# Pairs of small experts: first product from whole float32 weights, tokens stationary on two column tiles

## The chip, the cores and the metric

The kernel runs on one core of a Trainium2 chip. The metric is the time of one execution on the device, in microseconds (us), the median over several executions. Single runs of the kernel before lay between 1557.11 and 1559.25 us.

TensorE is called PE in the profile (PEld is its loading of stationary operands), VectorE is DVE, ScalarE is ACT, GpSimd is POOL, and SyncE is SP, whose queue issues nearly all transfers.

## The reference, cut to what matters

One decoder layer on 512 tokens of width 1024: attention in two head groups, then a mixture of 32 experts of which each token takes 4, then a gated per-layer input and a norm. The change touches the mixture alone:

```python
def expert_block(args):
    e, xs = args
    hh = jnp.dot(xs, w_gu[e]) + b_gu[e]            # w_gu[e]: 1024 x 2048
    glu, lin = jnp.split(hh, 2, axis=-1)
    glu = jnp.minimum(glu, SWIGLU_LIMIT)
    lin = jnp.clip(lin, -SWIGLU_LIMIT, SWIGLU_LIMIT)
    act = glu * jax.nn.sigmoid(SWIGLU_ALPHA * glu) * (lin + 1.0)
    return jnp.dot(act, w_dn[e]) + b_dn[e]         # w_dn[e]: 1024 x 1024
```

All weights are float32: 12 MB for an expert.

## The kernel before, in words

The attention part lasts some 310 us and isn't touched. After it the experts are ordered by how many tokens they have, and each place in that order has a fixed capacity (`CAPS`, line 34): 128 tokens for the first six, falling to 64 for the last twelve. `RUNS` (line 42) lists the order of work. There are 26 runs, counted from 0: twenty with one expert each, and six pairs of two experts with 64 tokens each. The pairs are runs 1, 2, 6, 11, 18 and 25, the last. A run whose tokens don't fit is completed later by `overflow`.

**Weights.** An expert's weights are 12 chunks of 1 MB (128 partitions x 2 x 1024, `chunk_views`, line 738): q 0 to 3 are the gate half of the first product, 4 to 7 the linear half, 8 to 11 the down product. `jobs` (line 752) lists all chunks in the order of their loading; for a pair first expert 0's eight, then expert 1's eight, then the down chunks of both by turns. `issue` (line 774) gives each next chunk to a free one of 8 raw slots and issues the load on SP's queue; the load waits until the last reader of the slot is done. From run 23 on, two of the slots are kept for something else, so 6 are left. In run 25 four chunks of the later gate projection (`("t", q)`) stand in the list between the first product and the down product.

A chunk is then either split or native. `advance` (line 798) splits a chunk into two float16 parts, high and low, in two halves (`hl`, line 210: ACT writes the high part in line 212, DVE the low one in line 213), into one of 6 places (`HL`), and its raw slot is free again. `take` (line 826) runs splits up to `AHEAD` = 4 chunks past the one that is needed. Native chunks (`native`, line 766, by `NATIVE`, line 38: the last 4 of an expert with 64 tokens, the last 2 of other small ones) are multiplied as float32 from the raw slot, which is free after that (`done`, line 832).

**One run.** `prep` (line 1407) gathers the tokens by matmuls with one-hot matrices (`gather`, line 1232; line 1245) into `xT`, tokens along the free axis, in two float16 parts; this is written in the program between the first product and the down product of the run before. `up` (line 1268) does the first product for one expert: the bias (line 1279), then for each k and each of eight blocks of 128 outputs three matmuls (`mm3`, lines 218 to 220: high x high, low x high, high x low) with the weights stationary and the tokens moving; the result has outputs on partitions and tokens along the free axis. Gate and linear parts meet in lines 1298 to 1303. In a pair `up` runs twice, once for each expert. Then the down product: `down` (line 1307) for a single run, `down2` (line 1329) for a pair. `down2` takes whole float32 weights as moving operand, 512 columns at a time, and the activations as stationary operand; expert 0 writes PSUM partitions 0 to 63, expert 1 partitions 64 to 127, two column tiles of PE.

`y_out` (line 1341) scales the result into two float16 parts. Every third run, `combine` (line 1350) adds the results of the last three runs to the output by matmuls (line 1358); its eight pieces are spread over the first product of the next run by `step` (line 1366), one after each k. `at` (line 1415) puts small extra work (the sort, the down bias) at fixed points of some runs.

The framework may move instructions between places of the program where data allow; waits are kept by semaphores.

Of the kernel before, what the change touches and what calls it, by code (L numbers as in the profile page):

```python
# [19 lines left out]
P = 128  # L20
# [14 lines left out]
MAXBLK = 48  # L35
GROUP = 3
AHEAD = 4
NATIVE = {c: 0 if c == 128 else 4 if c <= 64 else 2 for c in CAPS}
SHIFT = 1200


# [7 lines left out]
def hybrid_layer(ctx: ExitStack, tc: tile.TileContext, x, p, positions, w_in, g_attn, g_cq, w_uq, g_ckv,  # L49
# [703 lines left out]
    for n_, us in enumerate(RUNS):  # L753

        if n_ == LAST - 1:
            jobs += [("t", 4), ("t", 5)]
        jobs += [(s_, q) for s_ in us for q in range(8)]
        if n_ == LAST:
            jobs += [("t", q) for q in range(4)]
        jobs += [(s_, q) for q in range(8, 12) for s_ in us]  # L760
# [546 lines left out]
    def down(y, get, put, acts, c):  # L1307

        split_acts = {}
        t = mp.tile([P, 2, 2, 4, P], F16, name="acts", bufs=1)  # L1310
        for q in range(4):
            slot, w = get(8 + q)
            j = q // 2
            if slot is not None and j not in split_acts:
                split_acts[j] = [t[:, j, b, :, :c] for b in range(2)]
                hl(*split_acts[j], acts[j], SX / S)
            for m in range(q % 2 * 2, q % 2 * 2 + 2):
                for n in range(2):
                    first, end = q == 0 and m == 0, q == 3 and m == 3
                    cols = slice(n * 512, (n + 1) * 512)  # L1320
                    if slot is None:
                        PE.matmul(y[n][:c], acts[j][:, m], w[:, m % 2, cols], start=first, stop=end,  # L1322
                                  skip_group_check=True)
                    else:
                        ah, al = split_acts[j]
                        mm3(y[n][:c], ah[:, m], al[:, m], w[0][:, m % 2, cols], w[1][:, m % 2, cols], first, end)
            put(8 + q)

    def down2(y, get, put, acts):

        for q in range(4):
            ws = [get(e, 8 + q)[1] for e in range(2)]
            for m in range(2):
                for n in range(2):
                    for e in range(2):
                        PE.matmul(y[n][e * 64:(e + 1) * 64], acts[e][:, 2 * q + m], ws[e][:, m, n * 512:(n + 1) * 512],  # L1336
                                  start=q + m == 0, stop=q + m == 4, skip_group_check=True)
            for e in range(2):
                put(e, 8 + q)

    def y_out(y, gcl, c):
        yh = mp.tile([P, D], F16, name="yh", tag="yh", bufs=4)
# [64 lines left out]
    def prep(us, between=None, mid=None):  # L1407
        n, s_ = len(us), us[0]
        pos, X_ = (posf, X3) if s_ < 2 else (XP, XS)
        oh = onehots(pos[:, :, s_:s_ + n], n * CAPS[s_], n)  # L1410
        if between is not None:
            between()
        return gather(oh, lambda i: X_[:, i, 0:2, s_:s_ + n], n * CAPS[s_], n, mid=mid)

    def at(ns_, k):
        for f in extra.pop((ns_, k), ()):
# [28 lines left out]
    for ns_, us in enumerate(RUNS):  # L1445
# [5 lines left out]
        if ns_ == LAST - 2:  # L1451
            later["keep"] = 2
        perm = st256 if us[0] < 2 else perm256
        acts = []

        def get(e, q):
            return take((us[e], q))

        def put(e, q):
            done((us[e], q))  # L1460

        for j in range(len(us)):
            acts += up(lambda q: get(j, q), lambda q: put(j, q), xT, j * c, perm[:, us[j]:us[j] + 1], c)
            at(ns_, j + 1)
        if len(us) == 1:
            at(ns_, 2)
        if ns_ + 1 < len(RUNS):
            nxt = prep(RUNS[ns_ + 1])
        y = [py_.tile([P, 512], F32, name="y", tag="py") for _ in range(2)]
        if ns_ == LAST:  # L1470
            step(99)
        if len(us) > 1:
            down2(y, get, put, acts)
        else:
            down(y, lambda q: get(0, q), lambda q: put(0, q), acts, c)
        at(ns_, 3)
# [121 lines left out]
```

## Time and profile before

| | |
|---|---|
| median of 3 executions | 1559.07 us |
| the profiled execution's own time | 1560.22 us |
| its span, first to last instruction | 1558.3 us |
| mean granted clock of PE | 0.97 of full speed |
| read from memory | 427.99 MB |
| mean rate over the span | 278 GB/s |

The span is the stretch that the trace shows, the profiled execution's own time has what lies around it. Runs 0 to 25 fill the trace from about 320 to 1492 us. In the views a row has a line of the kernel, an engine, an operation, what it writes and reads, and how often it stands there. Busy time of PE counts matmuls that overlap in the array once, so a busy PE need not be at its best rate; the number of matmuls in a stretch tells more. "Issue" is time in which an engine waited for nothing that the profile shows.

### The profile page before, as it was taken

How to read it: one execution, taken by the hardware profiler on the slowest of the kernel's cores; microseconds unless marked ns; L12 is line 12 of the kernel's file. 1: busy time of each engine (PE TensorE's matmuls, PEld its weight loads, DVE VectorE, ACT ScalarE, POOL GpSimd, SP SyncE). 2: the span in 40 equal slices, each digit the busy share in tenths (PEclk: the TensorE clock that was granted, in tenths of full speed). 3: DMA queues.
4: the chain of work that ended last, by engine and by line, in shares of the span. 5: the costliest groups of instructions: out<-in, count | busy, mean ns of one | idle time of the engine just before them, and what ended most of it. 6: DMA issues, size and time to landing. Idle time of an engine off the chain costs nothing. (4 is left out here: it accounts for less than half of the span.)

```text
span 1558.3 us, 44542 instructions
## 1 busy us (share of the span) xinstructions
PE 1401.5 (90%) x19286; PEld 1016.2 (65%) x19286; DVE 1175.4 (75%) x1624; ACT 980.8 (63%) x1393; POOL 45.0 (3%) x114
## 2 busy tenths in 40 slices
PE   7999899688889999899997999998987898899587
PEld 4766656486565787688776577676665566556447
DVE  7447876788595999599987387887857777788734
ACT  6458866567374887488675366766646646567534
POOL 2001000300000000000000000000000000000002
PEclk9999999889999999999999999999999899999799
DMA  7122131368899999799999699999987999788911
GB/s 246 46 85 83 55 109 44 119 227 277 317 399 368 408 407 344 267 382 408 342 356 349 216 405 367 399 334 344 351 312 290 391 354 340 279 322 317 330 69 55
DMA packets 124249, 433.00 MB, mean 278 GB/s; under 512 B 7977, under 2 KB 18770, under 8 KB 123986
## 3 DMA queue, kind: packets, MB, share of 16 engines
q1 hardware_dynamic: 123858, 429.85, 74.1%
q8 instruction: 153, 2.51, 0.6%
q14 instruction: 46, 0.38, 0.1%
q10 hardware_dynamic: 192, 0.26, 0.1%
HBM read 427.99 MB, written 2.10 MB: 276 GB/s over the span
## 5 line engine op out<-in xcount | busy, mean ns | idle before, releaser
L213 DVE SCALAR_TENSOR_TENSOR hl<-raw,hl 128x1024 f16<-128x1024 f32 x618 | 721.8, 1216 | 52.5 <-ACT hl L212 49.4
L212 ACT ACTIVATE hl<-raw 128x1024 f16<-128x1024 f32 x618 | 611.0, 1048 | 96.3 <-DMA raw<-in_w_gu_dram 57.8
L220 PE MATMUL hps<-xT,hl 128*128 128x64 f16 (+5 forms) x4096 | 501.2, 204 | 28.0 <-issue 13.4
L218 PE MATMUL hps<-xT,hl 128*128 128x64 f16 (+5 forms) x4096 | 504.6, 204 | 12.8 <-issue 11.1
L219 PE MATMUL hps<-xT,hl 128*128 128x64 f16 (+5 forms) x4096 | 503.7, 204 | 12.4 <-issue 12.4
L220 PEld LDWEIGHTS <-hl 128*128 128x128 f16 (+1 forms) x4208 | 400.3, 99 | 54.4 <-DVE hl L213 25.5
L219 PEld LDWEIGHTS <-hl 128*128 128x128 f16 (+1 forms) x4208 | 402.6, 99 | 38.7 <-issue 22.5
L218 PEld LDWEIGHTS <-hl 128*128 128x128 f16 (+1 forms) x4208 | 402.8, 99 | 33.9 <-issue 9.5
L1346 ACT ACTIVATE yh<-y,gcl 128x512 f16<-128x512 f32 (+4 forms) x52 | 35.1, 682 | 143.4 <-PE y L1336 69.3
L1347 DVE SCALAR_TENSOR_TENSOR yl<-y,gcl,yh 128x512 f16<-128x512 f32 (+4 forms) x52 | 38.3, 746 | 106.3 <-ACT yh L1346 104.4
L1336 PE MATMUL y<-raw,ln 128*64 128x512 f32 x384 | 101.2, 606 | 10.9 <-DVE ln L1299 10.4
L1247 ACT ACTIVATE xT<-pg 128x512 f16<-128x512 f32 (+4 forms) x104 | 53.1, 522 | 91.3 <-PE pg L1245 90.5
L1322 PE MATMUL y<-raw,ln 128*80 128x512 f32 (+3 forms) x224 | 98.6, 592 | 0.0
L218 PE MATMUL y<-hl,acts 128*128 128x512 f16 (+4 forms) x208 | 82.5, 397 | 5.9 <-ACT acts L212 5.6
L1358 PE MATMUL pg<-yh,ohT 128*128 128x512 f16 (+4 forms) x208 | 80.8, 389 | 7.0 <-issue 5.1
L219 PE MATMUL y<-hl,acts 128*128 128x512 f16 (+4 forms) x208 | 81.7, 393 | 0.0
L220 PE MATMUL y<-hl,acts 128*128 128x512 f16 (+4 forms) x208 | 79.3, 392 | 2.6 <-DVE acts L213 2.0
L1358 PE MATMUL pg<-yl,ohT 128*128 128x512 f16 (+4 forms) x208 | 80.6, 389 | 0.7 <-DVE yl L1347 0.6
L1336 PEld LDWEIGHTS y<-raw,ln 128*64 128x64 f32 x384 | 32.0, 138 | 65.9 <-issue 51.7
L1322 PEld LDWEIGHTS y<-raw,ln 128*80 128x80 f32 (+3 forms) x224 | 35.0, 157 | 55.0 <-issue 52.9
L1358 PEld LDWEIGHTS <-ohT 128*128 128x128 f16 (+4 forms) x416 | 37.7, 99 | 45.5 <-issue 16.3
L1303 ACT ACTIVATE glu<-glu 128x512 f32<-128x512 f32 (+4 forms) x52 | 28.1, 556 | 61.8 <-DVE glu L1302 61.6
(363 smaller groups left out, 2125.1 us busy)
## 6 DMA issues: line engine op xcount, KB each, us to landing
raw<-in_w_gu_dram SPq DMA_DIRECT2D x256, 1024.0 KB, 10.7
raw<-in_w_dn_dram SPq DMA_DIRECT2D x128, 1024.0 KB, 10.2
raw<-in_w_in_dram SPq DMA_DIRECT2D x2, 2048.0 KB
raw<-in_w_o_dram SPq DMA_DIRECT2D x2, 2048.0 KB
raw<-in_w_ple_gate_dram SPq DMA_DIRECT2D x4, 1024.0 KB
acc<-in_x_dram SPq DMA_DIRECT2D x4, 512.0 KB, 3.6
raw<-in_w_in_dram SPq DMA_DIRECT2D x4, 512.0 KB, 7.2
out_dram<-acc SPq DMA_DIRECT2D x8, 256.0 KB, 4.2
```

What stands on the lines that cost most here:

```text
L212: later["hl"] = (A.activation(hi, src, AF.Copy, scale=scale), V.scalar_tensor_tensor(lo, src, scale, hi, op0=OP.mult, op1=OP.subtract))
L213: V.scalar_tensor_tensor(lo, src, scale, hi, op0=OP.mult, op1=OP.subtract))
L218: PE.matmul(ps, ah, bh, start=first, stop=False, skip_group_check=True)
L219: PE.matmul(ps, ah, bl, start=False, stop=False, skip_group_check=True)
L220: PE.matmul(ps, al, bh, start=False, stop=last, skip_group_check=True)
L1247: A.activation((xT[:, h] if parts else xT)[:, q * 4:(q + 1) * 4, :c], ps[:, :4 * c].rearrange("p (k c) -> p k c", k=4), AF.Copy, scale=1.0 ...
L1303: A.activation(t, t, AF.Gelu_apprx_sigmoid)
L1322: PE.matmul(y[n][:c], acts[j][:, m], w[:, m % 2, cols], start=first, stop=end, skip_group_check=True)
L1336: PE.matmul(y[n][e * 64:(e + 1) * 64], acts[e][:, 2 * q + m], ws[e][:, m, n * 512:(n + 1) * 512], start=q + m == 0, stop=q + m == 4, skip_ ...
L1346: A.activation(yh[:c, s_], y[n][:c], AF.Copy, scale=gcl[:c])
L1347: V.scalar_tensor_tensor(yl[:c, s_], y[n][:c], gcl[:c], yh[:c, s_], op0=OP.mult, op1=OP.subtract)
L1358: PE.matmul(ps, ohT[:c, i * P:(i + 1) * P], y_[:c, n * 512:(n + 1) * 512], start=e == 0 and q == 0, stop=e == last and q == 1)
```

## The change

Three things. `NATIVE` becomes 12 for experts with up to 64 tokens, so that no chunk of a pair is split. The list of loads takes the first product's chunks of a pair by turns. And the first product of a pair is done by `up2` in place of two calls of `up`: tokens are the stationary operand (`xT`, now gathered as one float32 matrix, `parts=False`), the weights move 512 columns at a time, and the two experts are on two column tiles, as in the down product. `pair_mm` is that loop, for both products. As the result then has tokens on partitions, `turn2` turns it by eight transposes on PE and two copies on ACT before the down product. `step` is called after each pair of chunks. Single runs keep their path.

```diff
-NATIVE = {c: 0 if c == 128 else 4 if c <= 64 else 2 for c in CAPS}
+NATIVE = {c: 0 if c == 128 else 12 if c <= 64 else 2 for c in CAPS}
...
-        jobs += [(s_, q) for s_ in us for q in range(8)]
+        jobs += [(s_, q) for q in range(8) for s_ in us]
...
-    def down2(y, get, put, acts):
-
+    E2 = [slice(e * 64, (e + 1) * 64) for e in range(2)]
+
+    def pair_mm(ps, xT, k0, q, get, put, opened):
+
+        ws = [get(e, q)[1] for e in range(2)]
+        for m in range(2):
+            k = k0 + m
+            for n in range(2):
+                for e in range(2):
+                    PE.matmul(ps[n][E2[e]], xT[:, k, E2[e]], ws[e][:, m, n * 512:(n + 1) * 512],
+                              start=not opened and k == 0, stop=k == KD - 1, skip_group_check=True)
+        for e in range(2):
+            put(e, q)
+
+    def up2(get, put, xT, brows, mid):
+
+        for a in range(2):
+            ps = [ph_.tile([P, 512], F32, name="hps2", tag="ph") for _ in range(2)]
+            for n in range(2):
+                for e in range(2):
+                    PE.matmul(ps[n][E2[e]], brows[e].to_broadcast([P, 64]),
+                              btab[:, a * D + n * 512:a * D + (n + 1) * 512], start=True, stop=False,
+                              skip_group_check=True)
+            for q in range(4):
+                pair_mm(ps, xT, 2 * q, 4 * a + q, get, put, True)
+                step()
+            if a == 0:
+                r = []
+                for h in ps:
+                    t = mp.tile([P, 512], F32, name="glu", bufs=2)
+                    V.tensor_scalar(t, h, 1.0 / S, 7.0, op0=OP.mult, op1=OP.min)
+                    A.activation(t, t, AF.Gelu_apprx_sigmoid)
+                    r.append(t)
+                mid()
+        for n, h in enumerate(ps):
+            t = mp.tile([P, 512], F32, name="ln", bufs=2)
+            V.tensor_scalar(t, h, 7.0 * S, -7.0 * S, op0=OP.min, op1=OP.max)
+            V.scalar_tensor_tensor(t, t, S, r[n], op0=OP.add, op1=OP.mult)
+            r[n] = t
+        return r
+
+    def turn2(acts):
+
+        t = mp.tile([P, KD, P], F32, name="actT", tag="acts", bufs=1)
+        for n in range(2):
+            ps = pg()
+            for f in range(4):
+                PE.transpose(ps[:, f * P:(f + 1) * P], acts[n][:, f * P:(f + 1) * P], identf)
+            A.activation(t[:, 4 * n:4 * n + 4].rearrange("p f t -> p (f t)"), ps, AF.Copy)
+        return t
+
+    def down2(y, get, put, actT):
         for q in range(4):
...
+            pair_mm(y, actT, 2 * q, 8 + q, get, put, False)
...
-        return gather(oh, lambda i: X_[:, i, 0:2, s_:s_ + n], n * CAPS[s_], n, mid=mid)
+        return gather(oh, lambda i: X_[:, i, 0:2, s_:s_ + n], n * CAPS[s_], n, parts=n == 1, mid=mid)
...
-            down2(y, get, put, acts)
+            down2(y, get, put, turn2(acts))
```

## Rows read from the trace of the kernel before

**Rows 1.** Part 1 of the page: busy time, share of the span, instructions

```profile
PE 1401.5 (90%) x19286; PEld 1016.2 (65%) x19286; DVE 1175.4 (75%) x1624; ACT 980.8 (63%) x1393; POOL 45.0 (3%) x114
```

**Rows 2.** Timeline of ACT: first eviction of the run before each pair (start, duration)

```profile
370.99 1.25 ACT L1346 ACTIVATE yh<-y,gcl 128x512 f16<-128x512 f32 x2
...
423.90 1.25 ACT L1346 ACTIVATE yh<-y,gcl 128x512 f16<-128x512 f32 x2
...
607.63 1.25 ACT L1346 ACTIVATE yh<-y,gcl 128x512 f16<-128x512 f32 x2
...
823.54 0.69 ACT L1346 ACTIVATE yh<-y,gcl 112x512 f16<-112x512 f32 x1 [4.89 <-PE y L1322]
...
1107.37 0.68 ACT L1346 ACTIVATE yh<-y,gcl 80x512 f16<-80x512 f32 x1 [4.27 <-PE y L1322]
...
1423.28 0.68 ACT L1346 ACTIVATE yh<-y,gcl 72x512 f16<-72x512 f32 x1 [1.10 <-PE y L1322]
```

**Rows 3.** Line 1336 (down2) by pair: duration ns min/median/max, first to last start

```profile
L1336 PE MATMUL y<-raw,ln x64: 592/592/643, 408.3 to 423.0; 128*64 128x512 f32 x64
...
L1336 PE MATMUL y<-raw,ln x64: 592/592/643, 467.2 to 483.9; 128*64 128x512 f32 x64
...
L1336 PE MATMUL y<-raw,ln x64: 592/592/643, 650.1 to 664.8; 128*64 128x512 f32 x64
...
L1336 PE MATMUL y<-raw,ln x64: 592/592/643, 864.3 to 882.9; 128*64 128x512 f32 x64
...
L1336 PE MATMUL y<-raw,ln x64: 592/592/644, 1151.9 to 1176.2; 128*64 128x512 f32 x64
...
L1336 PE MATMUL y<-raw,ln x64: 592/592/1112, 1463.7 to 1491.2; 128*64 128x512 f32 x64
```

**Rows 4.** Groups by line and shape: busy us, mean ns | idle before, releasers

```profile
L213 DVE SCALAR_TENSOR_TENSOR hl<-raw,hl 128x1024 f16<-128x1024 f32 x618 | 721.8, 1216 | 52.5 <-ACT hl L212 49.4 <-PE hps L220 1.1
L212 ACT ACTIVATE hl<-raw 128x1024 f16<-128x1024 f32 x618 | 611.0, 1048 | 96.3 <-DMA raw<-in_w_gu_dram 57.8 <-PE hps L220 11.3 <-PE hps L219 8.8
L220 PE MATMUL hps<-xT,hl 128*128 128x64 f16 x1536 | 153.3, 197 | 18.7 <-issue 12.3 <-DVE hl L213 5.7
```

**Rows 5.** Windows in run 6: us, PE, PEld, DVE, ACT, POOL; PEclk, DMA share, GB/s

```profile
624.00:628.00 4.00, 4.00 (x143) 4.00 (x141) 4.00 (x5) 3.70 (x5) 0.00 (x0) 1.00 0.72 254
...
636.00:640.00 4.00, 2.85 (x98) 2.73 (x93) 4.00 (x5) 0.33 (x1) 0.00 (x0) 1.00 1.01 384
```

**Rows 6.** Timeline of run 6's down product: loads of the stationary operand (start, us)

```profile
656.21 0.14 PEld L1336 LDWEIGHTS y<-raw,ln 128*64 128x64 f32 x2 [0.28 <-issue]
...
657.50 0.14 PEld L1336 LDWEIGHTS y<-raw,ln 128*64 128x64 f32 x2 [0.29 <-issue]
```

**Rows 7.** Window in run 2, line 1336 alone: us, PE, PEld, PEclk, DMA share, GB/s

```profile
472.00:482.00 10.00, 10.00 (x50) 4.01 (x48) 1.00 1.02 410
```

**Rows 8.** Timeline of PE, four places (start, us)

```profile
297.78 0.73 PE L627 MATMUL tp<-identf,acc 128*128 128x128 f32 x4
...
859.21 0.97 PE L1245 MATMUL pg<-oh,sqh 128*128 128x96 f16 x19
...
876.15 0.35 PE L1279 MATMUL hps<-perm,btab 128*128 128x96 f16 x4
...
878.29 0.35 PE L1279 MATMUL hps<-perm,btab 128*128 128x96 f16 x4
```

**Rows 9.** Line 1358 (combine) in run 6's first product

```profile
L1358 PE MATMUL pg<-yh,ohT x24: 379/379/380, 608.4 to 623.4; 128*128 128x512 f16 x24
```

**Rows 10.** DMA issues: a single load of 1 MB, us to landing

```profile
raw<-in_w_ukv_dram SPq DMA_DIRECT2D x1, 1024.0 KB, 4.8
```

**Rows 11.** Waits in run 25, 1455 to 1495 us

```profile
PE y L1336 <- DVE ln L1299: 10.2, 1, 10.2
```

**Rows 12.** Window in run 11's first product, columns as in rows 5

```profile
836.00:840.00 4.00, 2.39 (x45) 2.39 (x46) 4.00 (x5) 2.60 (x4) 0.00 (x0) 0.67 1.03 410
```

More of the change, by code (lines that the diff above doesn't have):

```diff
@@ L1309, in down @@
         split_acts = {}
-        t = mp.tile([P, 2, 2, 4, P], F16, name="acts", bufs=1)
+        t = mp.tile([P, 2, 2, 4, P], F16, name="acts", tag="acts", bufs=1)
         for q in range(4):
@@ L1327, in down @@
             put(8 + q)
-    def down2(y, get, put, acts):
-        for q in range(4):
[L1332 to L1339, printed above, removed]
+    E2 = [slice(e * 64, (e + 1) * 64) for e in range(2)]
@@ L1453, in hybrid_layer @@
         perm = st256 if us[0] < 2 else perm256
-        acts = []
         def get(e, q):
@@ L1460, in put @@
             done((us[e], q))
-        for j in range(len(us)):
-            acts += up(lambda q: get(j, q), lambda q: put(j, q), xT, j * c, perm[:, us[j]:us[j] + 1], c)
-            at(ns_, j + 1)
+        brows = [perm[:, s_:s_ + 1] for s_ in us]
         if len(us) == 1:
-            at(ns_, 2)
+            acts = up(lambda q: get(0, q), lambda q: put(0, q), xT, 0, brows[0], c)
+            at(ns_, 1)
+        else:
+            acts = up2(get, put, xT, brows, lambda: at(ns_, 1))
+        at(ns_, 2)
         if ns_ + 1 < len(RUNS):
```

## The prediction

> **What bounds the kernel now.** I read the shares of the whole page first, then the stretches of the six pairs, then what each engine does and waits for inside them. Over the span TensorE (PE) is busy most, VectorE (DVE) next [rows 1]; a share does not say which one a pair waits for, so I cut the pairs out. A pair begins when the run before it hands over its result, the first eviction of that run [rows 2], and ends with its last float32 matmul of the down product [rows 3]. From these, in the order of time, with the run's place in the list: run 1 takes 52.0 us (423.0 less 371.0), run 2 60.0, run 6 57.2, run 11 59.4, run 18 68.8, run 25 67.9; the mean is 60.9. Up to the first down matmul, which I call the front, they take 37.3, 43.3, 42.5, 40.8, 44.5 and 40.4.
>
> The change works on the front alone. Before, it needs 32 splits (16 chunks in two halves) on DVE at 1.216 and on ACT at 1.048 [rows 4]: 38.9 us of DVE for a pair, some of it done ahead. It needs 768 matmuls of 64 columns on PE. In a full stretch 143 of them pass in 4.00 us, 28 ns each, so 21.5 us. Later in the same pair only 98 pass while DVE is busy without a gap [rows 5]: there the splits set the pace. The small matmuls also wait by themselves, "issue" 12.3 us on one of the three lines [rows 4]. So a front of 37 to 44 us holds 21.5 us of first product, and the rest is the room that the change may win.
>
> **The change part by part.**
>
> *Removed:* the splits of 16 chunks in a pair, 38.9 us of DVE and 33.5 of ACT, and 768 matmuls, 21.5 us of PE at their best.
>
> *Added, first product:* 8 k x 2 parts x 2 column halves x 2 experts = 64 float32 matmuls, which the trace shows as two records each, as it does for the 32 of the down product (64 records a pair, [rows 3]). That product has the same shape and the same two column tiles, so its rate is the price: the loads of two records follow each other every 0.43 us, three steps in 1.29 [rows 6], 0.215 a record. 128 records are **27.5 us**, 6.0 above the best case of before. Weights stream from the same buffers while transfers run at 410 GB/s and still 50 records pass in 10 us [rows 7], so no price is added for that. Bias: 8 matmuls of 512 columns, two at a time, 0.9 us, against 32 x 0.028 = 0.9: nothing.
>
> *Added, the turn:* eight float32 transposes, four in 0.73 us with their latency [rows 8], and two copies on ACT. Before, nothing stood here. The rows of before show no such turn inside a pair, so I bound it: nothing, if the gather of the next run (5.1 us from 859.21 to the first down matmul at 864.3, [rows 3, 8]) hid all; 4 us, if two transposes' groups, two copies of the length of an eviction (0.69, [rows 2]) and DVE's last step ran one after another. The limiting steps on DVE (two of about an eviction's length for each half) lie under the gather, the first four transposes and the first copy don't: 0.73 + 0.69 + hand-over, **2 us**. Queued behind the copies on ACT are the next run's splits, which wait for transfers anyhow. In run 25 there is no gather to hide DVE's steps.
>
> *Gather and gates:* the gather keeps its 64 matmuls and loses two of four evictions on ACT, which lie under PE; nothing. Gelu and limits are as many as before. If DVE were still full they would cost, but the splits that filled it are gone.
>
> *Combine:* runs 6 and 18 carry the sums of a group of three in their first product. These last from 608.4 to 623.4 with 24 of 48 matmuls on this line [rows 9]; 48 of 512 columns at 0.214 are 10.3 us, as before. New is that each of eight pieces now stands between matmuls on column tiles. Four bias matmuls of a later run show such a visit: 876.15 and again 878.29 [rows 8], 2.14 apart, with eight float32 records (1.72) and four short matmuls (0.17) in between, so 0.25 is lost in a round trip: 8 x 0.25 = **2 us**.
>
> *Moved, the transfers:* chunks now alternate between the experts, and SP's next load into a slot is released by PE's matmul, not by DVE's split. The lead shrinks: 8 raw slots and the 4 split chunks ahead were 12 chunks, now 8 (6 in run 25). A chunk is 1.0486 MB, at 410 GB/s [rows 7] 2.56 us; one alone takes 4.8 to land [rows 10]. Matmuls eat a chunk in 1.72, so after the first 8 the pair may run at the transfers' pace. The Trainium skill (DMA: Bandwidth & Descriptors, Specifications) gives an HBM limit of about 358 GB/s for a core; by it 24 chunks would take 70.3 us, 9.4 above the mean pair, and the six would cost 56 us more. The row with 410 GB/s speaks against it, so the sum leaves it out.
>
> Matmuls alone give a front of 0.7 (handing over) + 0.9 + 27.5 + 5.1 + 2 = **36.2 us**. By pair:
> - Run 1: a first quarter frees its two slots 4.4 us after 371.0, two chunks land 7.4 later, then two every 5.1: the last up chunks at about 398, the front ends about 1.5 after the matmuls' 36.2, at 37.7. About 0.
> - Run 2: of the 48 chunks of runs 1 and 2, 40 must come after the first slot is free at 375.4: 375.4 + 2.2 + 40 x 2.56 = 480, then one quarter of 3.4 us: 483.4, against 483.9 now [rows 3]. 0.
> - Run 6: 36.2 + 10.3 + 2 = 48.5 against 42.5. +6.0. The first product is slow enough here that transfers keep up.
> - Run 11: 36.2 and about 2 for the last chunks, 38.2 against 40.8. -2.6.
> - Run 18: 48.5, less 1.0 for a gather of 80 columns, 47.5 against 44.5. +3.0.
> - Run 25: 6 slots. 28 chunks (four are not the pair's), 22 of them after the first slot is free near 1428.9: 1428.9 + 2.2 + 22 x 2.56 = 1487.4, then 3.4: 1490.8, against 1491.2. 0, even though the stall of 10.2 us behind DVE's splits of those four [rows 11] may go: the last down chunk is late next.
>
> Sum +6.4: 1566.6 on the profiled execution's own 1560.2, which stands 1.15 above the median of the runs, so 1565 there. The down product, the other runs and the end keep their times: single runs are split and multiplied as before, and the four splits that they no longer do ahead for a pair ended under their own down product.
>
> **The rivals.**
>
> *Faster.* The one mechanism: transfers do not set the pace, because slots come free in time, and the stalls of before go as far as the matmuls allow. Run 1 wins 1.1, run 2 (with 3.4 for sixteen matmuls of the down bias, 0.214 each) 3.7, run 11 4.6, run 25 has neither gather nor stall: about 36.4 (sums of one run included) against 40.4, and 10.2 more, 14.2. With +9.0 in runs 6 and 18 this is -14.6: 1544. It decides at chunks nine to sixteen: if they land within 1.72 us each after the first eight are eaten. For it speaks that DVE paces the front now [rows 5]; against it the 2.56 us of a chunk.
>
> *No change.* A pair takes 60.9 us now, and 24 chunks at 2.56 are 61.4. If the pairs are held by transfers before and after, nothing moves: 1559 to 1562. Against it: runs 6 and 18 have 10 us of sums in them.
>
> *Much slower.* Where matmuls wait for chunks (3.4 of every 5.1 us busy), PE's clock may fall. In run 11 it stood at 0.67 in a stretch with 2.39 of 4.00 us busy [rows 12]. A quarter then takes 6.9 us instead of 5.1; over ten of the some twenty paced quarters that is 18 us: 1583. The share of 3.4 in 5.1 is above that row's, so it is unlikely. The Trainium skill (TensorE: Matmul & The Clock Gate, Part 1) says that the throttled clock is the default and activity releases it; by that the transfers' waits speak against this change, and the trace agrees with the row named.
>
> **How the numbers follow.** A difference of 0.2%, 3.1 us, is about what a measurement of this kernel tells from none. Forecast 0.43, much slower 0.07, faster 0.33, no change 0.17. So slower by over 0.2% has 0.50, within it 0.17, faster 0.33. The predicted time is the forecast's, 1565. Its own range: the turn from 0 to 4 in six pairs (-12 to +12) but hidden by transfers in half of them, so 6 either way: 1559 to 1571. As the cases lie on both sides, the range for 8 in 10 reaches past the faster case, to 1541, and up to the much slower one, 1583.
>
> **What would show it right or wrong.** Right: first product of 128 records at about 0.215 with no split beside it; DVE idle in the pairs; run 6 and run 18 longer by 6 and 3; transfers near 410 GB/s through run 2; matmuls of the first product waiting for w_gu transfers from the fifth quarter on; 2 us between gather and down product. Wrong: records that follow more slowly than 0.215; run 6 not longer, because sums fill waits; run 25 shorter by 10 or more; single runs next to a pair that change by more than 2 us; a clock below 1.00 in the pairs' fronts.

## The result, and the profile after

The changed kernel takes 1577.18 us (median of 4, 1575.16 to 1577.53), the kernel before 1559.16 on the same chip: 1.0108 of it, with a 95% interval from 1.0081 to 1.0134. It is slower by 1.1%, some 18 us; the two profiles differ by 15.1 us in their spans. Forecast were +6.4 us.

The head of the page of the changed kernel and its first part, against [rows 1]:

```profile
span 1573.4 us, 36005 instructions
PE 1454.3 (92%) x15350; PEld 930.3 (59%) x15350; DVE 961.4 (61%) x1432; ACT 797.1 (51%) x1201; POOL 45.0 (3%) x114
```

DVE lost 214 us of work and ACT 184, PE gained 53. What the change was to take away is gone, and the kernel is longer. Three groups of the table by line and shape, against [rows 4]:

```profile
L213 DVE SCALAR_TENSOR_TENSOR hl<-raw,hl 128x1024 f16<-128x1024 f32 x426 | 497.4, 1218 | 39.6 <-ACT hl L212 37.8 <-PE hps L220 1.2
...
L1340 PE MATMUL hps<-raw,xTf 128*64 128x512 f32 x768 | 191.1, 597 | 4.9 <-DMA raw<-in_w_gu_dram 4.9
...
L1340 PE MATMUL y<-raw,actT 128*64 128x512 f32 x384 | 109.7, 618 | 13.1 <-DMA raw<-in_w_dn_dram 9.9 <-ACT hl L212 2.2 <-ACT actT L1379 0.9
```

192 splits are gone, 32 in each of six pairs, as forecast. To see where the time went, I cut the trace again at the first eviction of each run. On ACT these stand in line 1391 now; the rows answer to [rows 2] (that of run 11 is left out), the second is the end of run 1 and the last one the end of run 25:

```profile
366.21 1.33 ACT L1391 ACTIVATE yh<-y,gcl 128x512 f16<-128x512 f32 x2 [7.17 <-PE y L220]
...
435.86 0.69 ACT L1391 ACTIVATE yh<-y,gcl 128x512 f16<-128x512 f32 x1 [2.90 <-PE y L1340]
...
615.77 1.33 ACT L1391 ACTIVATE yh<-y,gcl 128x512 f16<-128x512 f32 x2 [8.69 <-PE y L220]
...
1112.96 0.68 ACT L1391 ACTIVATE yh<-y,gcl 80x512 f16<-80x512 f32 x1 [10.16 <-PE y L1322]
...
1429.57 0.68 ACT L1391 ACTIVATE yh<-y,gcl 72x512 f16<-72x512 f32 x1 [10.16 <-PE y L1322]
...
1506.90 0.69 ACT L1391 ACTIVATE yh<-y,gcl 128x512 f16<-128x512 f32 x1 [18.73 <-PE y L1340]
```

From all 26 such rows of each kernel, in us, with the experiments that the text comes to below (the last four columns are later_first, lead, t_first and best3; "single" is the sum of the nineteen single runs after run 0, run 0 counts from the start of the trace):

| run | before | changed | fixed order, later expert first | lead of 14 | projection first | best (best3) |
|---|---|---|---|---|---|---|
| 0 | 371.0 | 366.2 | 364.8 | 367.2 | 367.3 | 366.9 |
| 1 | 52.9 | 69.7 | 59.9 | 47.3 | 69.9 | 47.3 |
| 2 | 59.8 | 56.6 | 56.5 | 67.0 | 56.7 | 56.8 |
| 6 | 56.9 | 60.7 | 60.7 | 60.7 | 60.7 | 59.3 |
| 11 | 59.2 | 58.0 | 54.3 | 51.6 | 57.8 | 49.9 |
| 18 | 68.6 | 72.0 | 64.3 | 78.6 | 72.0 | 65.5 |
| 25 | 67.7 | 77.3 | 74.7 | 69.5 | 62.7 | 62.2 |
| single | 754.9 | 746.5 | 749.0 | 750.8 | 749.9 | 744.0 |

The first two columns give the account of the 15.9 us up to the last eviction: the pairs take 29.1 us more, of which run 1 alone 16.7 and run 25 9.6; run 0 takes 4.8 less and the single runs 8.4 less. So the loss isn't spread evenly over the pairs; most of it stands in two places. The down product (line 1340, `pair_mm`) in runs 1, 6 and 25, against [rows 3]:

```profile
L1340 PE MATMUL y<-raw,actT x64: 592/592/644, 405.9 to 436.1; 128*64 128x512 f32 x64
...
L1340 PE MATMUL y<-raw,actT x64: 592/592/643, 663.3 to 676.7; 128*64 128x512 f32 x64
...
L1340 PE MATMUL y<-raw,actT x64: 592/592/1116, 1475.3 to 1507.1; 128*64 128x512 f32 x64
```

The same 64 records of a down product last 13.4 us in run 6, 30.2 in run 1 and 31.8 in run 25. Before, run 1 took 14.7 for them.

**Run 1.** The timeline of PE in its down product (start, duration):

```profile
405.91 1.93 PE L1340 MATMUL y<-raw,actT 128*64 128x512 f32 x4
407.77 0.32 PE L1197 MATMUL pg<-identf,binfo 128*128 128x128 f32 x1
408.03 3.65 PE L1340 MATMUL y<-raw,actT 128*64 128x512 f32 x12
...
411.97 1.19 PE L1218 MATMUL pg<-bd,XT 64*128 64x512 f16 x4
413.09 1.93 PE L1340 MATMUL y<-raw,actT 128*64 128x512 f32 x4
```

Each quarter is cut into a piece of 4 records and one of 12. The rows don't name the expert; the times say that the 4 are the first two matmuls of one expert, without their partners. They last 1.86 us to the next instruction, 0.465 a record, and the 12 take 3.58, which is four more without a partner (1.86) and eight by turns (1.72 at the 0.215 of [rows 6]). Sixteen by turns would take 3.44. The eight pieces add up to 21.8 us, 8 more than unbroken; in the other 8.4 of the 30.2 stand the row tables of `over_rows` (line 1197), the down bias (line 1218) and the gather of run 3, which is work moved here and not time lost. Busy time doesn't show this: PE is "busy" all the while.

**Run 25.** The DMA queue of SP, and PE's costliest wait there (us in total, times, longest):

```profile
1461.12 1.41 SPq L771 DMA_DIRECT2D raw<-in_w_ple_gate_dram  x2
1464.55 2.26 SPq L771 DMA_DIRECT2D raw<-in_w_dn_dram  x1
1476.16 3.56 SPq L771 DMA_DIRECT2D raw<-in_w_ple_gate_dram  x2
1479.97 13.88 SPq L771 DMA_DIRECT2D raw<-in_w_dn_dram  x7
```

```profile
PE y L1340 <- DMA raw<-in_w_dn_dram: 9.9, 4, 8.6
```

After the one chunk issued at 1464.6 nothing is issued until 1476.2, and seven of the eight down chunks come after that. PE waits, and there, and in no front of a pair, its clock falls. A window of 4 us (us, PE, PEld, DVE, ACT, POOL; PEclk, DMA share, GB/s):

```profile
1484.00:1488.00 4.00, 0.58 (x2) 0.30 (x4) 3.27 (x9) 3.29 (x9) 0.00 (x0) 0.50 1.00 380
```

### The profile page after: what moved, and what is told of

Same layout as the page of the kernel before. It is cut to its first block, busy times and chain, and to the rows that moved or that the text cites. A ratio compares the mean times of both kernels' runs of the same rounds, so it can differ in the third digit from the quotient of the medians.

```text
span 1573.4 us, 36005 instructions
## 1 busy us (share of the span) xinstructions
PE 1454.3 (92%) x15350; PEld 930.3 (59%) x15350; DVE 961.4 (61%) x1432; ACT 797.1 (51%) x1201; POOL 45.0 (3%) x114
## 5 line engine op out<-in xcount | busy, mean ns | idle before, releaser
L213 DVE SCALAR_TENSOR_TENSOR hl<-raw,hl 128x1024 f16<-128x1024 f32 x426 | 497.4, 1218 | 39.6 <-ACT hl L212 37.8
L212 ACT ACTIVATE hl<-raw 128x1024 f16<-128x1024 f32 x426 | 421.0, 1047 | 67.7 <-DMA raw<-in_w_gu_dram 41.4
L220 PE MATMUL hps<-xT,hl 128*128 128x128 f16 (+4 forms) x2560 | 348.4, 209 | 11.1 <-DVE hl L213 6.0
L218 PE MATMUL hps<-xT,hl 128*128 128x128 f16 (+4 forms) x2560 | 352.0, 209 | 4.1 <-ACT hl L212 3.2
L219 PE MATMUL hps<-xT,hl 128*128 128x128 f16 (+4 forms) x2560 | 351.3, 209 | 1.5 <-issue 1.5
L218 PEld LDWEIGHTS <-hl 128*128 128x128 f16 (+1 forms) x2672 | 262.6, 99 | 26.4 <-ACT hl L212 5.7
L220 PEld LDWEIGHTS <-hl 128*128 128x128 f16 (+1 forms) x2672 | 260.7, 99 | 26.5 <-DVE hl L213 13.1
L219 PEld LDWEIGHTS <-hl 128*128 128x128 f16 (+1 forms) x2672 | 262.7, 99 | 21.7 <-issue 7.5
L1340 PE MATMUL hps<-raw,xTf 128*64 128x512 f32 x768 | 191.1, 597 | 4.9 <-DMA raw<-in_w_gu_dram 4.9
L1340 PEld LDWEIGHTS hps<-raw,xTf 128*64 128x64 f32 x768 | 60.4, 136 | 114.5 <-issue 100.8
L1340 PE MATMUL y<-raw,actT 128*64 128x512 f32 x384 | 109.7, 618 | 13.1 <-DMA raw<-in_w_dn_dram 9.9
L1247 ACT ACTIVATE xT<-pg 128x512 f16<-128x512 f32 (+4 forms) x80 | 39.2, 501 | 137.8 <-PE pg L1245 136.9
L1405 DVE SCALAR_TENSOR_TENSOR acc<-pg,acc 128x512 f32<-128x512 f32 x80 | 53.9, 686 | 81.5 <-PE pg L1403 81.4
L1340 PEld LDWEIGHTS y<-raw,actT 128*64 128x64 f32 x384 | 33.8, 140 | 74.9 <-issue 55.5
```

The costliest lines, as they stand in the source:

```text
L212: later["hl"] = (A.activation(hi, src, AF.Copy, scale=scale), V.scalar_tensor_tensor(lo, src, scale, hi, op0=OP.mult, op1=OP.subtract))
L213: V.scalar_tensor_tensor(lo, src, scale, hi, op0=OP.mult, op1=OP.subtract))
L218: PE.matmul(ps, ah, bh, start=first, stop=False, skip_group_check=True)
L219: PE.matmul(ps, ah, bl, start=False, stop=False, skip_group_check=True)
L220: PE.matmul(ps, al, bh, start=False, stop=last, skip_group_check=True)
L1247: A.activation((xT[:, h] if parts else xT)[:, q * 4:(q + 1) * 4, :c], ps[:, :4 * c].rearrange("p (k c) -> p k c", k=4), AF.Copy, scale=1.0 ...
```

## The experiments

Each ratio is to the kernel before, on the same chip in the same hour. Where there is no ratio, places of the trace are compared: run 6 takes 60.69 to 60.71 in every kernel whose change doesn't reach it, so tenths of a microsecond can be read there. Other places move more from trace to trace: run 0 lies between 364.8 and 367.3 and the sum of the single runs between 744.0 and 750.8 in the kernels with the changed first product and whole loads. A kernel's whole time moves by more still: the kernel before spread from 1558 to 1571 us in the executions beside the experiments, so a difference of two traces and one of two ratios need not agree.

**pin: a fixed order.**

```diff
+        last = None
...
-                    PE.matmul(ps[n][E2[e]], xT[:, k, E2[e]], ws[e][:, m, n * 512:(n + 1) * 512],
+                    i = PE.matmul(ps[n][E2[e]], xT[:, k, E2[e]], ws[e][:, m, n * 512:(n + 1) * 512],
...
+                    if last is not None:
+                        behind(i, last)
+                    last = i
```

> The changed kernel, but with the matmuls of each pair of chunks held in the written order (expert 0 and expert 1 by turns). Theory 'order': in run 1 the down product of the changed kernel goes through one expert's chunk in pieces of 4 and 12 records, which take 1.86 and 3.58 us (four of each, 21.8 us) in place of 64 records at 0.215 (13.7 us), because only one column tile is at work in them. With the experts by turns it loses 8 us of its 30.1 us (405.9 to 436.0); run 2 waits for transfers and may give back up to half of it: the kernel becomes 4 to 8 us shorter, about 1571. Rival 'transfers': run 1 is long because chunks arrive late; then the same waits show at other matmuls and the kernel stays within 1.5 us of 1577. Rival 'visits': it is the other work between the pieces (bias of the down product, transposes, gather: some 9 us) that lengthens it; then run 1 keeps its 69.7 us and the kernel its time.

Ratio 1.0025 (1.0006 to 1.0044). Run 1 falls by 4.3 us to 65.3, run 18 by 2.8, run 11 by 1.4, the trace by 7.0 up to its last eviction (the two ratios, 1.0108 and 1.0025, stand some 13 us apart). The order matters, but only half of the 8 us came back in run 1, since the quarters are still cut. The timeline of PE there:

```profile
411.50 1.07 PE L1341 MATMUL y<-raw,actT 128*64 128x512 f32 x2
...
414.79 3.65 PE L1341 MATMUL y<-raw,actT 128*64 128x512 f32 x14
```

One matmul alone (2 records) takes 1.07, and the other 14 take as long as 16 do, since one of the other expert's is left without its partner: a matmul alone costs no less than the two by turns.

**later_first: the fixed order, later expert first.**

```diff
-                for e in range(2):
+                for e in (1, 0):
```

> The changed kernel with the fixed order of the matmuls, but in it the expert whose chunk is loaded second comes first. So far the first matmul of a quarter was ready one transfer before the second, and the framework put other work between the two: a quarter of 16 records was cut into 2 and 14 (1.07 and 3.65 us) or into 4 and 12 (1.86 and 3.58). Now each quarter should stand in one piece of 16 in 3.65. Theory 'one column tile at work': the down product of run 1 falls by another 4 x 1.0 us, run 1 from 65.3 (fixed order) to 61 or 62, run 18 and run 11 by 1 to 3 us; the kernel ends 3 to 7 us before the one with the fixed order, near the kernel before (0.998 to 1.001 of it). Rival 'transfers': with 8 slots the runs are held by loads; the waits come back at the first matmul of each quarter, run 1 and run 2 together keep 121, and the kernel stays at 1.0025.

Ratio 0.9971 (0.9953 to 0.9989): this alone turns the loss into a small gain. Run 1 takes 59.9, run 18 64.3 (72.0 in the changed kernel), run 11 54.3. Each quarter stands in one piece:

```profile
402.68 3.65 PE L1341 MATMUL y<-raw,actT 128*64 128x512 f32 x16
406.27 1.03 PE L1218 MATMUL pg<-bd,XT 64*128 64x512 f16 x4
...
409.33 3.65 PE L1341 MATMUL y<-raw,actT 128*64 128x512 f32 x16
```

The other work is still between the quarters, so it wasn't the visits that cost most, and transfers didn't take the gain back. The first product had lost its rate in the same way. The groups of this run, against 191.1 and 109.7 in the changed kernel:

```profile
L1341 PE MATMUL hps<-raw,xTf 128*64 128x512 f32 x768 | 173.0, 596 | 11.7 <-DMA raw<-in_w_gu_dram 11.6
...
L1341 PE MATMUL y<-raw,actT 128*64 128x512 f32 x384 | 89.1, 612 | 11.0 <-DMA raw<-in_w_dn_dram 10.9
```

That is 38.7 us of busy time less, of which 22.6 reach the last eviction. Part of the rest had filled waits for chunks: in these two groups PE now waits 22.5 us for transfers, in the changed kernel 14.8. In the second half of run 2's first product such waits now stand open, and run 2 takes 56.5 as it did:

```profile
447.71 3.65 PE L1341 MATMUL hps<-raw,xTf 128*64 128x512 f32 x16 [1.39 <-DMA raw<-in_w_gu_dram]
452.83 3.65 PE L1341 MATMUL hps<-raw,xTf 128*64 128x512 f32 x16 [1.47 <-DMA raw<-in_w_gu_dram]
```

Why the framework cut the quarters can't be read from a trace; that the cut goes when the expert loaded last comes first fits an order that counts on one chunk landing before the other.

**old25: the last pair as before.** Run 25 takes the order of loads, the four native chunks an expert, `up` and the down product of the kernel before.

```diff
+OLD = {25}
...
+        elif ns_ in OLD:
+            acts = []
+            for j in range(2):
+                acts += up(lambda q: get(j, q), lambda q: put(j, q), xT, j * c, brows[j], c)
+                at(ns_, j + 1)
...
-            down2(y, get, put, turn2(acts))
+            down2_old(y, get, put, acts) if ns_ in OLD else down2(y, get, put, turn2(acts))
```

> The changed kernel, but the last pair (run 25) goes the way of the kernel before: split chunks, loads of expert 0 first, no turn. Theory 'queue': run 25 lost 9.6 us (77.3 against 67.7) since the splits of four chunks of the later projection stand on ACT behind a copy of the turn that waits 23.6 us for PE, so their raw slots come free late and the down chunks are loaded late. Then this run takes 67.7 again and the kernel ends 9 to 10 us earlier, 1567 to 1568. Rival 'transfers': run 25 is long because the transfers were behind by then (the stretch of run 24 read at 267 GB/s against 325); then run 25 keeps 3 us or more of the loss and the kernel is at 1570 or above.

Ratio 1.0029 (1.0012 to 1.0046); run 25 takes 66.6, 10.7 less. The place was right. The cause named in this expectation was not, as the next run shows.

**no_turn: no transposes, no copies.**

```diff
...
-            down2(y, get, put, turn2(acts))
+            down2(y, get, put, acts)
```

> The changed kernel without the turn: the eight transposes and two copies are left out and the down product takes the unturned activations as stationary operand, of the same shape. Run 6 (60.70 in every run so far, before 56.94) tells the price of the turn: by the forecast 2.0 us, so 58.7; by the gap that the trace shows between the gather and the down product (661.6 to 663.3) 1.7 us. If the rise of run 6 were all the turn's, it would fall to 57. Run 25 tells the queue on ACT: by 'queue' (a copy of the turn waits 23.6 us on ACT with the splits of the later projection's chunks behind it) it falls from 77.3 to 69 or less; by the rival, that the transfers are simply behind in run 25, it falls by the turn's 2 to 3 us only, to 74 to 75.

One execution, 1575.47 us. Run 6 falls by 1.1 us to 59.6, but that isn't the turn alone. Without it the down product of run 6 is cut, and 1.2 us of bias matmuls for run 7 (line 1279) move behind it. The pieces here, then the transposes of the changed kernel:

```profile
656.41 1.07 PE L1340 MATMUL y<-raw,ln 128*64 128x512 f32 x2
...
660.28 1.08 PE L1340 MATMUL y<-raw,ln 128*64 128x512 f32 x4
...
661.62 13.09 PE L1340 MATMUL y<-raw,ln 128*64 128x512 f32 x58
```

```profile
661.93 0.66 PE L1378 MATMUL pg<-identf,ln 128*128 128x128 f32 x4
...
662.65 0.65 PE L1378 MATMUL pg<-identf,ln 128*128 128x128 f32 x4
```

The pieces take 1.15 us more than 64 records in one, and about cancel the bias; the transposes take 0.49 and 0.68 to the next instruction, 1.17 in all, with no idle time of PE behind them. So 1.1 is near the turn's price in run 6. In the other five pairs the time changes by -3.2 (run 11) to +1.0 (run 18), with other cuts. Run 25 keeps 77.4, so the theory of ACT's queue falls. The splits of the first two chunks of the later projection on ACT and the loads on SP now:

```profile
1468.91 6.49 ACT L212 ACTIVATE hl<-raw,gw 128x256 f16<-128x256 f32 x16 [20.86 <-DMA raw<-in_w_ple_gate_dram]
```

```profile
1463.69 2.31 SPq L771 DMA_DIRECT2D raw<-in_w_dn_dram  x1
1474.83 3.54 SPq L771 DMA_DIRECT2D raw<-in_w_ple_gate_dram  x2
1478.62 12.42 SPq L771 DMA_DIRECT2D raw<-in_w_dn_dram  x7
```

The first two chunks, issued at 1460.3, land and are split by 1475.4; only as their slots come free (1474.8) are the second two issued, and the down chunks stand behind them on SP.

**t_first: the later projection's chunks ahead of the last pair.**

```diff
-        jobs += [(s_, q) for q in range(8) for s_ in us]
         if n_ == LAST:
             jobs += [("t", q) for q in range(4)]
+        jobs += [(s_, q) for q in range(8) for s_ in us]
```

> The changed kernel, but the four chunks of the later projection are loaded and split before the last pair's chunks, not between its two products. Without the turn run 25 kept 77.4 us, so it isn't the copies on ACT. New theory 'a load bound to a slot that waits for a split': the second two of the four chunks are put into the slots of the first two, which must land and be split first (1461 to 1476), and seven down chunks stand behind these loads on SP's queue. Then run 25 falls from 77.3 to 60 to 67 us, the stretch before it reads at more than 267 GB/s, and the kernel ends at 1562 to 1567. Rival 'six slots': in run 25 only six slots are left, and no order of loads helps; then it keeps 73 us or more.

Run 25 takes 62.7, 14.6 less, in the middle of what was expected; run 24 reads at 320 GB/s in place of 267. Ratio 1.0009 (0.9991 to 1.0027), the kernel before within the error. SP's queue flows:

```profile
1403.71 9.14 SPq L771 DMA_DIRECT2D raw<-in_w_ple_gate_dram  x4
...
1464.69 20.28 SPq L771 DMA_DIRECT2D raw<-in_w_dn_dram  x8
```

**lead: 14 chunks.** Chunks of a pair's first product also go into free places for split chunks, seen as float32, once all earlier chunks that need a split have theirs.

```diff
...
-            f = rawfree.pop(0)
-            raws[s_, q] = f, raw_slot(f, views[s_][q])
+            if rawfree:
+                f = rawfree.pop(0)
+                raws[s_, q] = f, raw_slot(f, views[s_][q])
+            else:
+                f = hlfree.pop(0)
+                v = HL[:, f].bitcast(F32).rearrange("p (a b) -> p a b", a=2)
+                SY.dma_start(v, views[s_][q])
+                raws[s_, q] = ("h", f), v
...
```

> The changed kernel, but chunks of a pair's first product may also be loaded into the six places for split chunks, which stand empty in a pair, when the eight raw slots are full: up to 14 chunks ahead in place of 8. Theory 'lead': between 354 and 371 us the changed kernel reads nothing (0 to 6 GB/s), as all slots hold chunks that PE has not reached; 16 us are six chunks at 2.56. With places for them runs 1 and 2, which end at 492.4, end 8 to 12 us earlier, at 480 to 484, run 25 gains some us too, and the kernel comes to 1563 to 1569. Rival 'order': transfers are not what lengthens runs 1 and 2, only the pieces of the down product in which one column tile works; then they end within 3 us of 492.4 and the kernel stays at 1574 or above. Run 6, which waits for no transfer, keeps 60.7 by both.

Ratio 0.9979 (0.9960 to 0.9998); run 2 ends at 481.5, run 25 takes 69.5. The window ahead of run 1, first of the changed kernel, then of this one:

```profile
362.00:366.00 4.00, 4.00 (x20) 1.76 (x19) 0.00 (x0) 0.00 (x0) 0.00 (x0) 1.00 0.00 0
```

```profile
362.00:366.00 4.00, 4.00 (x20) 1.86 (x19) 0.00 (x0) 0.00 (x0) 0.00 (x0) 1.00 0.98 334
```

The transfers go on where they stood. But the edit also moved the framework's order: run 1's down product now stands unbroken, the down bias moved into run 2 (67.0), and run 18 was cut in more places than in the changed kernel and takes 78.6. So its 14 us in all are not a clean price of the lead; runs 1 and 2 together, 11.9 us less, are the better figure, and best2 below bears it out.

```profile
401.34 13.95 PE L1351 MATMUL y<-raw,actT 128*64 128x512 f32 x64
```

**half_after and half_before: transfers nearly free.** Both kernels load only one of the two rows a partition of an expert's chunk once a slot has been filled, and leave the rest as an earlier chunk left it.

```diff
-        SY.dma_start(v, ap)
+        if half and s_ in full:
+            SY.dma_start(v[:, :1], ap[:, :1])
+        else:
+            SY.dma_start(v, ap)
+        full.add(s_)
...
```

> The changed kernel; of each expert chunk only the first 128 of 256 rows are loaded after a slot's first use (the other rows keep what an earlier chunk left there), so 0.52 in place of 1.05 MB; matmuls and splits stay as they are. It tells what the kernel takes when transfers are nearly free. Theory 'order and queue': the losses of run 1's down product (8 us) and of run 25's chain lie in orders of work, so the changed kernel stays longer than the kernel before with the same halved loads, by 8 to 18 us. Rival 'transfers': the losses come from chunks that land late (lead of 8 in place of 12), so with halved loads the changed kernel is as fast as the kernel before with halved loads, or faster by up to 15.

> The kernel before with the same halved loads, as the other half of that comparison. If transfers hold back single runs and pairs (runs 13 to 16 show 406 to 408 GB/s), it falls by 20 to 60 us below 1559. If splits on DVE and matmuls on PE set the time nearly everywhere, it falls by less than 10. The difference to the changed kernel with halved loads is what tells: 8 to 18 us in favour of the kernel before by 'order and queue', none or the other sign by 'transfers'.

0.9640 (0.9603 to 0.9678) and 0.9654 (0.9620 to 0.9687): the two kernels are equal when loads are halved. By the letter that speaks for 'transfers'. It doesn't settle it, as in half_after the down products of all six pairs came out unbroken (64 records in 13.95 us); lighter loads change the order as well. What the two do show: the pairs still take 8.0 us more than before (335.3 against 327.3), run 6 and run 18 4 to 5 each, while run 0 takes 4.7 and the single runs 9.9 less. These gains stay when the loads are halved.

**visits: sums by two.**

```diff
-                step()
+                step(2 * (q % 2))
```

> The changed kernel, but the eight pieces of the sums of a group stand two together after every second pair of chunks of a first product: four visits between matmuls on column tiles in place of eight. By the forecast a visit costs 0.25 us, so run 6 falls from 60.70 by 1.0 to 59.7, and run 18 the same. If visits cost nothing, 60.7 stays. If the whole rise of run 6 over before (3.8) came from visits, it would fall by 1.9.

Run 6 falls by 1.4 to 59.3. The timeline of PE in its first product, of the changed kernel and of this one (six sums' matmuls after each 16 records, twelve after each 32):

```profile
616.77 3.60 PE L1340 MATMUL hps<-raw,xTf 128*64 128x512 f32 x16
...
626.69 3.65 PE L1340 MATMUL hps<-raw,xTf 128*64 128x512 f32 x16
```

```profile
616.55 7.03 PE L1340 MATMUL hps<-raw,xTf 128*64 128x512 f32 x32
626.21 7.09 PE L1340 MATMUL hps<-raw,xTf 128*64 128x512 f32 x32
```

32 records and 12 sums' matmuls take 9.92 with two visits and 9.66 with one: 0.26 a visit. Four of them are 1.0 of the 1.4; the rest lies in the gather, which the framework cut once less. Run 18 became 1.2 longer, and the kernel as a whole gained nothing (one execution, 1578.13 us).

**best1: three edits.** The order of pin, the lead of 14, and ACT's copies of the turn held behind the projection's splits in run 25 (`after` is ACT's last split there).

```diff
...
-            A.activation(t[:, 4 * n:4 * n + 4].rearrange("p f t -> p (f t)"), ps, AF.Copy)
+            i = A.activation(t[:, 4 * n:4 * n + 4].rearrange("p f t -> p (f t)"), ps, AF.Copy)
+            if after is not None:
+                behind(i, after)
...
```

> Three edits together: experts by turns in the fixed order (which gave 1.0025 in place of 1.0108 against before), 14 chunks of lead, and in run 25 the copies of the turn held behind the splits of the later projection's chunks on ACT. If the three losses are separate: runs 1 and 2 end near 478, run 25 takes about 70, and the kernel ends 10 to 15 us before the one with the fixed order alone, some 0.5% under the kernel before: 1549 to 1555 on a chip where before takes 1559. Rival: the losses overlap (runs 1 and 2 are held by 410 GB/s whatever the order, and run 25 by its six slots); then it gains under 5 us on the fixed order and stands at 1.000 to 1.003 against before.

Ratio 0.9904 (0.9882 to 0.9926): faster than both kernels. Runs 1 and 2 end at 475.7, run 25 takes 70.4, run 18 is still cut (73.8).

**best2 and best3: the causes that held.** Of the edits shown above, best2 joins those of later_first, lead and t_first; best3 has that of visits as well.

> Three edits together: the later expert first in a fixed order, 14 chunks of lead, the later projection's chunks before the last pair. If the three causes are separate, runs 1 and 2 take 105 to 110 us together (126.2 in the changed kernel, 112.7 before), run 18 about 70, run 25 60 to 65: 1536 to 1543 where the kernel before takes 1559, 0.983 to 0.989 of it. Rival: 14 chunks of lead already hide the cuts and run 25's loads; then it stands no better than the earlier sum of three edits, 0.990.

> The same three edits, and the pieces of a group's sums by two after every second pair of chunks. Four visits fewer took 1.4 us from run 6, but run 18 was 1.2 longer. If a visit costs 0.36 us wherever it is, this ends 2 to 3 us before the version with three edits. Rival: in run 18 transfers take it back, and the two are within 1 us.

best2: 0.9755 (0.9732 to 0.9778), median 1523.81. best3: 0.9739 (0.9719 to 0.9760), median **1521.34**, where the kernel before takes 1563.49. That is more than I expected. Runs 1 and 2 together take 104.1, 22.1 less than in the changed kernel; the order alone gave 9.8 and the lead 11.9, so the two edits add up. The lead had moved the order too, so its own price is better read from later_first to best2, where no quarter of the down products of runs 1 and 2 is cut in either: 12.3. Run 25 takes 62.2. The first part of the page of best3:

```profile
PE 1407.9 (93%) x15350; PEld 916.9 (60%) x15350; DVE 960.5 (63%) x1432; ACT 793.8 (52%) x1201; POOL 45.0 (3%) x114
```

The same 15350 matmul records as in the changed kernel, in 46 us less of busy time, 44 of them at the two products of the pairs: matmuls of one tile alone and a low clock had been counted as work. Between best2 and best3 the intervals overlap; by the traces run 6 gains 1.4 and run 18 0.3.

## Why the prediction was right or wrong

The sign and the range held, but much of that is luck. The pairs took 29.1 us more where 6.4 were forecast, and the rest of the kernel 13.2 less where nothing was: two errors of opposite sign, which left 1565 only 12 us low. By the prediction's own steps:

- **The rate of the product, 27.5 us a pair: right where the tiles alternate, short elsewhere.** A window in run 6's first product, where [rows 5] showed DVE without a gap, has 20 records in 4 us with no split beside them:

```profile
648.00:652.00 4.00, 4.00 (x20) 1.17 (x16) 0.00 (x0) 0.00 (x0) 0.00 (x0) 1.00 1.03 410
```

Over all six pairs the records keep PE busy for 191.1 us, 31.9 a pair, and with the later expert first for 173.0, 28.8 a pair. The sum had nothing for a tile that works alone.
- **The turn, 2 us: too dear.** 1.2 in run 6, by the timeline of the changed kernel.
- **Visits, 0.25 each: the number right, its working wrong.** The sums taken by two give 0.26. But the prediction took it from 2.14 us of [rows 8] "with eight float32 records (1.72)", and the timeline there has four:

```profile
876.43 1.93 PE L1336 MATMUL y<-raw,ln 128*64 128x512 f32 x4
```

They last 1.86 us to the next instruction, 0.465 each. So the rows chosen as a sign of a small visit were one column tile at work alone, which is what lengthened run 1.
- **Run 6, +6.0; run 18, +3.0.** Measured +3.8 and +3.4. Run 6 was near for partly wrong reasons: the front grew from 42.5 to 47.5 (48.5 forecast), and the down product, now in one piece, lasts 1.3 less than before, which the sum had left as it was. Run 18's figure agrees by chance: its front grew by 5.4 us, from 44.5 to 49.9, and its down product lasts 22.3 against 24.3. With quarters in one piece the run takes 64.3, 4.3 less than before.
- **"The down product [...] keep their times": the step that failed.** The sum took the rate of an unbroken down product, gave it to the first product too, and let every down product keep its time. The rate depends on the order in which the framework puts the two experts' matmuls and what it puts between them, and the change moved both. In run 1 the product took 30.2 us for 14.7, and quarters in one piece return 9.8 us in runs 1 and 2. The rows that the prediction rests on could have said so: in [rows 3] the same 64 records last 14.7 us in runs 1 and 6 and 24.3 in run 18, and the timeline of PE of the kernel before shows the same cut there:

```profile
1151.93 1.93 PE L1336 MATMUL y<-raw,ln 128*64 128x512 f32 x4
...
1154.12 3.65 PE L1336 MATMUL y<-raw,ln 128*64 128x512 f32 x12
```

So the kernel before pays in run 18 what the changed one pays in run 1. Neither the fixed order, which would serve its down product as well, nor the earlier place of the later projection's chunks was tried on the kernel before; so how much of the best version's 2.6% is due to the change isn't shown.
- **Lead and transfers: the mechanism right, the price too small in runs 1 and 2.** The lead did shrink, and transfers ran at 406 to 416 GB/s from 452 us to the end of run 2, as forecast. But runs 1 and 2 were put at no change; they rose by 13.5 (run 1 16.7 more, run 2 3.2 less). The sum counted from the first slot freed at 375.4 and left out that, with an order that eats slots late, the transfers would pause inside run 1 too: from 418 to 450 us they ran at 276 GB/s. With both causes gone the two runs take 104.1 us, 8.6 less than before. The promised sign, waits from the fifth quarter on, was hidden in the changed kernel, whose first product in run 2 has 31.8 us of matmuls and 1.0 of waiting for chunks. With the later expert first the same product has 28.4 and 4.3, the waits stand ahead of the sixth to eighth quarter, and these start 5.12 us apart, as the forecast 5.1. So matmuls of one tile alone had stood where PE would have waited.
- **Run 11, -2.6: half of it.** -1.2 measured, -9.3 in the best version.
- **Run 25, 0: wrong, +9.6.** "The last down chunk is late next" was right, and its date wrong. The 2.56 us a chunk assumed that SP issues as soon as any slot is free. It issues in order, and two loads at its head were bound to slots that first had to be filled and split. With the order of loads changed, run 25 takes 62.7.
- **"The other runs [...] keep their times": wrong, -13.2.** Run 0 takes 4.8 less and the single runs 8.4. In run 0 the splits done ahead for the pair did not end under its own down product: from 320 us to its end DVE was busy for 43.1 us before and for 32.0 now, and the waits of PE's down product on the activations' parts fell from 2.2 to 1.2. PE also idled less, and kept its clock; before and changed, columns as in [rows 5]:

```profile
350.00:360.00 10.00, 7.13 (x62) 4.84 (x59) 8.89 (x15) 3.39 (x5) 0.00 (x0) 0.66 0.71 250
```

```profile
350.00:360.00 10.00, 8.81 (x102) 5.79 (x99) 6.16 (x14) 3.05 (x5) 0.00 (x0) 1.00 0.35 124
```

No run parts the share of the clock from that of the waits. The single runs moved both ways; run 7, behind a pair, takes 2.6 more, which was one of the signs of being wrong. Their sum gains as much with halved loads, so the amount read from memory hardly explains it; which wait went is open.
- **The much slower rival.** It didn't come; the change went the other way. Before, the granted clock over the fronts of runs 1, 11, 18 and 25 was 0.95, 0.92, 0.96 and 0.92; in the changed kernel the mean is 1.00 in all six, and within the pairs it fell only in run 25's down product, where PE stood still. The Trainium skill (TensorE: Matmul & The Clock Gate, Part 1) says that the throttled clock is the default; the trace agrees with it in that place, a granted clock of 0.50, half speed, from 1484 to 1488.

## What to carry to other kernels

A rate read from one stretch holds for a stretch with the same order of instructions, not for the same instructions: where two column tiles share PE, look in the timeline whether the tiles alternate, since busy time hides it, and hides with it that PE would otherwise wait for a load. Where the framework orders an engine's work, an edit to one stage moves others; hold the order by hand where the rate hangs on it, with the operand that lands last in front. And in a ring of slots, ask to which slot each load is bound and what must happen before it is free: the queue that issues in order makes every later load wait too.

## What the runs showed of the hardware beyond the forecast

One column tile at work alone took 1.86 us for 4 records (0.465 each), two by turns 0.215 a record, and a single matmul without its partner 1.07 us, after which 14 records still took the 3.65 of 16. The Trainium skill (TensorEngine Tiling (Array Packing), Tiling Modes) says that tiles operate independently and can work in parallel; the trace agrees where the two alternate, and shows that matmuls of one tile in a row don't get the other's time. The best version reads at 402 GB/s through the whole of run 2, with one core at work. The Trainium skill (DMA: Bandwidth & Descriptors, Specifications) gives a limit of about 358 GB/s for a core; the measurement lies above it here.
